# A two-layer encoder block: the order of the MLP's tiles, one pinned group of sums, and two diagonal matrices made earlier

## The chip, the cores and the metric

The kernel runs on one core of one Trainium2 chip, as one launch. The metric is the time of an execution in microseconds (us) on the device; the time before is the median of three runs. A profile is one further execution, recorded by the hardware profiler. Engines are named as in the profile: PE is TensorE (PEld its weight loads), DVE VectorE, ACT ScalarE, POOL GpSimd, SP the engine whose queue issues the loads of weights.

## What is computed

The reference is a stack of two layers over 256 tokens of width 2048. Each layer has an attention part and then an MLP; this case is about the MLP:

```
def sq_relu_mlp(h, g, w_in, w_out):
    return jnp.square(jax.nn.relu(rms_norm(h, g) @ w_in)) @ w_out

h = h + sq_relu_mlp(h, norm_mlp[layer], w_mlp_in[layer], w_mlp_out[layer])
```

`w_in` is 2048 x 8192 and `w_out` 8192 x 2048, all in fp32. `rms_norm` divides each token by the root of its mean square (plus 1e-6) and multiplies by a gain.

## The kernel before

**Precision.** Every fp32 operand is split into a high part, rounded by ACT (a cast to `float32r`), and a low part, the rest, which DVE subtracts. A product then takes three matmuls: high by high, high by low, low by high. Weights arrive as units of 128 x 1024 fp32 (512 KB, one DMA on SP's queue), are cast (hi) and subtracted (lo), and wait in rotating buffers: 6 raw, 4 hi, 5 lo. `weights()` hands out the next unit and prepares units ahead (`AHEAD = 3`), in the order of a list, `stream`, which is built from the same steps as the work. The lines of the splits are L171 and L174 (plain units, of up tiles), L225 and L226 (of sevens, with L220 to L224 as sums of the blocks first), L247 and L248 (of direct pairs).

**The MLP in steps.** The 8192 hidden features are four chunks of 16 tiles of 128. An up tile (a step "U" with its number, `features_major`) makes one tile of a chunk: 16 wide matmuls of 512 columns (high weights by both parts of the activations) and 16 narrow ones of 256 columns (low weights), all into one PSUM bank. Then `up` empties the bank: L449 on ACT copies one half, L1169 on DVE adds the other. `finish` follows: L1151 (DVE, ReLU and the tokens' inverse root), L1154 (ACT, square), and the split into `hid` by L1109 (ACT) and L1110 (DVE). For odd tiles below ten `block_sums` also forms sums of blocks (L1132 to L1135) and splits them.

The down projection of a chunk is two groups (n = 0 and 1), each of two column groups of 512. In a group, tiles 0 to 9 are taken two at a time by a seven ("S0" to "S4"): seven products in place of eight, Strassen's scheme in Winograd's form, 21 matmuls. Tiles 10 to 15 are taken directly: "A5" to "A7" for the first column group, "B5" to "B7" for the second, 12 matmuls each; A6 reads the tiles 12 and 13. A group has eight sums in PSUM: 11, 21 and 12 in the pool `acc` (four banks, the fourth is for up tiles), p1, p5 and 22 in a pool of two, p6 and p7 in pools of one. When the last product of a sum is in, it is copied or added (L1075, L1077) to sums in SBUF: four final ones per group, and `e`, the stored products of p1 with p6, p5 and p7.

**What sets the order.** `TURNS` writes the order of the steps by hand. The first string is the turn of group 0, in which the rest of the same chunk's up tiles is made; the second is the turn of group 1, in which the next chunk's first ten are made. The first string runs four times in a layer, the second three times (the last chunk's second group is computed afterwards by `tokens_major` or `features_major`). All TensorE instructions are kept in this order. For the other engines the framework simulates the program's time when it is built and orders each engine's instructions by that, so one that has its operands early can float ahead of where the program has it. `pin(ins)` keeps an instruction behind the one that the program has just before it on its engine: an order, not a wait.

**Side work.** A step ends in one or two calls of `slot()`, which advances each generator in `active` to its next `yield`. `merged(n)` adds the stored products of group n to the final sums, six additions of 128 x 512 (L1022), two to a slot; `merged(1)` is started in the last chunk before B5 (L1204), `merged(0)` by `merge_first` after the last step. `turned` then transposes the sums on TensorE and adds them to the residual stream (L1006). `inverse_root`, started four slots into the MLP, computes the inverse root of each token's mean square: two small matmuls (`stat`), a power on POOL (L553), two yields, then two diagonal matrices `dg` by DVE (L559), each followed by a matmul that spreads its diagonal over all partitions (`inv`, L560), and the copy `ri` that L1151 reads (L562).

Of the kernel before, what the change touches and what calls it, by code (L numbers as in the profile page):

```python
# [9 lines left out]
F32 = mybir.dt.float32  # L10
F32R = mybir.dt.float32r
AF = mybir.ActivationFunctionType
ALU = mybir.AluOpType
# [3 lines left out]
P = 128  # L17
D = 2048
T = 256
# [26 lines left out]
SEVEN = 5  # L46
ALONE = 10
TURNS = (
    "U10 S0 U11 S1 U12 A5 S2 U13 S3 A6 U14 S4 U15 B5 B6 A7 B7",
    "U0 S0 A5 U1 S1 A6 U2 S2 A7 U3 U4 S3 U5 U6 S4 U7 B5 U8 B6 U9 B7",  # L50
)


# [50 lines left out]
def trunk(  # L104
# [17 lines left out]
    nc = Engines(tc)  # L122
# [8 lines left out]
    nar = ctx.enter_context(tc.tile_pool(name="nar", bufs=6))  # L131
# [15 lines left out]
    ident = const.tile([P, P], F32, name="ident")  # L147
    make_identity(tc.nc, ident[:])
    neg_ones = const.tile([P, P], F32, name="neg_ones")
# [137 lines left out]
    def mm(o, lhs, rhs, start, stop):  # L287
        nc.tensor.matmul(o, lhs, rhs, start=start, stop=stop)
# [164 lines left out]
    def pin(ins, pinned=True):  # L453

        if pinned:
            tc.keep_in_program_order(ins)
# [88 lines left out]
    def inverse_root(acc, name):  # L545

        ps = ps_y.tile([P, 512], F32, name="stat", tag="y")
        for m in range(2):
            mm(ps[:, 2 * m : 2 * m + 2], acc[:, m * P : (m + 1) * P], neg_ones[:, 0:2], True, True)
        ms = tiny.tile([P, 4], F32, name="ms", tag="t4", bufs=8)  # L550
        nc.vector.tensor_scalar(ms[:], ps[:, 0:4], -1.0 / D, EPS, op0=ALU.mult, op1=ALU.add)
        r = tiny.tile([P, 4], F32, name="root", tag="t4", bufs=8)
        nc.gpsimd.tensor_tensor(r[:], ms[:], neg_half[:], op=ALU.pow)  # L553
        yield
        yield
        ps = ps_y.tile([P, 512], F32, name="inv", tag="y")
        for m in range(2):
            dg = nar.tile([P, P], F32, name="dg", tag="nar")
            nc.vector.tensor_scalar_mul(dg[:], ident[:], r[:, 2 * m : 2 * m + 1])  # L559
            mm(ps[:, m * P : (m + 1) * P], neg_ones[:], dg[:], True, True)  # L560
        ri = const.tile([P, T], F32, name=f"ri_{name}", tag="ri")
        nc.vector.tensor_scalar_mul(ri[:], ps[:, :T], -1.0)  # L562
        inverses[name] = ri
# [415 lines left out]

    def mlp(l, xg_, sq, h, done):  # L980
        start_side(delayed(inverse_root(sq, f"mlp{l}"), 4))
        sums = [heads4(f"d{l}_{i}") for i in range(4)]

        def summed(m, g):

            return sums[2 * m + g // 2][:, (g % 2) * 512 : (g % 2 + 1) * 512]
# [3 lines left out]
        def product_sum(i, n):  # L990

            return extra[i][:, n * 512 : (n + 1) * 512]
# [18 lines left out]
        def merged(n):  # L1011

            u, p5, p7 = (product_sum(i, n) for i in range(3))
            for i, (dst, src) in enumerate((
                (summed(0, 2 * n + 1), u),
                (summed(0, 2 * n + 1), p5),
                (u, p7),
                (summed(1, 2 * n), u),
                (u, p5),
                (summed(1, 2 * n + 1), u),  # L1020
            )):
                nc.vector.tensor_tensor(dst, dst, src, op=ALU.add)  # L1022
                if i % 2 == 1:
                    yield

# [151 lines left out]
        def merge_first(staged=staged):  # L1177
            if l == 1:
                yield from turned(3, None)
            for i, (dst, src) in enumerate(staged or ()):  # L1180
                nc.vector.tensor_tensor(dst, dst, src, op=ALU.add)
                if i % 2 == 1:
                    yield
            yield from merged(0)
            yield from turned(0, done)
            yield
            yield from turned(1, done)

        groups = {}
        for c, n, kind, i in mlp_steps():  # L1190
            if kind == "H":
                halves_first(xg_, FIRST_UP, lambda f, b: up(0, f, b))
                continue
            if kind == "T":
                two_tiles(xg_, [lambda b, f=f: up(0, f, b) for f in (i, i + 1)])
                continue
            if kind == "U":
                width["last"] = "wide"
                features_major(xg_, lambda b, c=c, i=i: up(c, i, b))
                continue  # L1200
            if (c, n) not in groups:
                groups[c, n] = Group(c, n, chunks[c][1], staged if c == NCH - 1 else None)
            if (c, kind) == (NCH - 1, "B") and i == sevens:
                start_side(merged(1))  # L1204
            if kind == "S":
                groups[c, n].seven(i)
            else:
                groups[c, n].direct(i, "AB".index(kind) + 1)
# [217 lines left out]
```

## Time and profile before

| | us |
|---|---|
| median of three runs | 2193.57 (2192.35 to 2194.9) |
| the profiled execution, its own time | 2191.9 |
| its span, first to last instruction | 2190.2 |
| PE busy | 2156.7 |
| DVE busy | 1743.2 |
| ACT busy | 1248.8 |
| MLP of the first layer, from its first up tile to its last matmul | about 435 to 1125 |
| MLP of the second layer | about 1483 to 2187 |

A row of the waits view reads: the waiting engine, its tile and line, the awaited engine, tile and line, then the idle time in all, how often, and the longest. All matmuls carry the line of a wrapper, L75, so they are told apart by tiles: `acc<-mlpx,hi` and `acc<-mlpx,lo` are the wide and narrow halves of up tiles, `acc<-hi,hid` and its like belong to sevens and direct pairs. A row of the timeline reads: start, duration, engine, line, operation, tiles, shape, count, and in brackets the engine's idle time before it and what ended that. Matmuls are pipelined: one of 512 columns lasts 0.39 us, and the next starts well before it ends. Times in a view are us from the span's start.

### The profile page before, as it was taken

How to read it: one execution, taken by the hardware profiler on the slowest of the kernel's cores; microseconds unless marked ns; L12 is line 12 of the kernel's file. 1: busy time of each engine (PE TensorE's matmuls, PEld its weight loads, DVE VectorE, ACT ScalarE, POOL GpSimd, SP SyncE). 2: the span in 40 equal slices, each digit the busy share in tenths (PEclk: the TensorE clock that was granted, in tenths of full speed). 3: DMA queues.
4: the chain of work that ended last, by engine and by line, in shares of the span. 5: the costliest groups of instructions: out<-in, count | busy, mean ns of one | idle time of the engine just before them, and what ended most of it. 6: DMA issues, size and time to landing. Idle time of an engine off the chain costs nothing.

```text
span 2190.2 us, 30309 instructions
## 1 busy us (share of the span) xinstructions
PE 2156.7 (98%) x11038; PEld 1841.7 (84%) x11038; DVE 1743.2 (80%) x2603; ACT 1248.8 (57%) x1828; POOL 205.2 (9%) x223
## 2 busy tenths in 40 slices
PE   9999999999999999999999999999999999999999
PEld 8888888888888888888888888888888888888887
DVE  7778886679888898899885556566988888888985
ACT  7644445456666555565555447555666656555563
POOL 0010112500000000000050112361000000000000
PEclk9999999999999999999999999999999999999999
DMA  9655556655665666656756654465665665666574
GB/s 330 194 162 184 172 182 197 194 176 182 197 211 182 198 189 197 201 188 183 207 175 192 191 188 130 135 190 181 188 203 185 197 193 191 194 193 211 164 218 129
DMA packets 213317, 414.65 MB, mean 189 GB/s; under 512 B 13232, under 2 KB 144304, under 8 KB 213168
## 3 DMA queue, kind: packets, MB, share of 16 engines
q1 hardware_dynamic: 212592, 410.63, 60.6%
q10 hardware_dynamic: 576, 2.10, 0.3%
q8 instruction: 86, 1.41, 0.3%
q14 instruction: 63, 0.52, 0.1%
HBM read 410.58 MB, written 2.10 MB: 188 GB/s over the span
## 4 chain that ended last, share of the span: by engine, by line
PE 93%; DVE 4%; issue 1%; DMA 1%; ACT 1%; DVEq 0%; ACTq 0%
PE acc L75 88%; PE accs L75 1%; PE yp L75 1%; DVE lo L226 1%; DVE lo L174 1%; PE tp L75 1%; DMA raw<-in_w_down 1%; PE s L75 1%; PE z L75 1%; DVE lo L248 0%; DVE raw L220 0%; ACT hi L225 0%; DVE up L1169 0%; DVE d L1022 0%; PE cold L75 0%
## 5 line engine op out<-in xcount | busy, mean ns | idle before, releaser
L174 DVE TENSOR_TENSOR lo<-raw,hi 128x1024 fp32r<-128x1024 f32 (+1 forms) x524 | 639.5, 1236 | 242.2 <-ACT hi L171 211.9
L171 ACT CAST hi<-raw 128x1024 fp32r<-128x1024 f32 (+1 forms) x524 | 541.4, 1043 | 345.0 <-PE acc L75 296.2
L75 PE MATMUL acc<-mlpx,hi 128*128 128x512 f32 x2048 | 485.5, 390 | 12.2 <-DVE up L1169 12.2
L75 PE MATMUL acc<-hi,hid 128*128 128x512 f32 x1404 | 473.6, 391 | 7.5 <-DVE hid L1110 6.7
L75 PEld LDWEIGHTS acc<-mlpx,hi 128*128 128x128 f32 x2048 | 382.7, 188 | 93.3 <-DVE up L1169 14.6
L225 ACT CAST hi<-raw 128x1024 fp32r<-128x1024 f32 (+1 forms) x280 | 264.5, 945 | 217.8 <-DVE raw L221 120.4
L226 DVE TENSOR_TENSOR lo<-raw,hi 128x1024 fp32r<-128x1024 f32 (+1 forms) x280 | 302.9, 1087 | 50.5 <-ACT hi L225 38.8
L75 PEld LDWEIGHTS acc<-hi,hid 128*128 128x128 f32 x1404 | 263.4, 188 | 63.5 <-DVE hid L1110 10.1
L75 PE MATMUL acc<-lo,hid 128*128 128x512 f32 x702 | 274.4, 391 | 0.0
L75 PEld LDWEIGHTS acc<-mlpx,lo 128*128 128x128 f32 x2048 | 261.3, 191 | 9.0
L75 PE MATMUL acc<-mlpx,lo 128*128 128x256 f32 x2048 | 264.6, 283 | 0.0
L75 PE MATMUL acc<-hi,xg 128*128 128x512 f32 x640 | 208.4, 398 | 0.0
L75 PEld LDWEIGHTS acc<-lo,hid 128*128 128x128 f32 x702 | 132.2, 188 | 23.7
L247 ACT CAST hi<-raw 128x1024 fp32r<-128x1024 f32 x108 | 113.6, 1055 | 61.7 <-PE acc L75 51.8
L248 DVE TENSOR_TENSOR lo<-raw,hi 128x1024 fp32r<-128x1024 f32 x108 | 131.6, 1230 | 20.7 <-ACT hi L247 20.6
L449 ACT COPY low<-acc 128x256 f32<-128x256 f32 x188 | 69.5, 370 | 137.7 <-PE acc L75 135.1
L75 PEld LDWEIGHTS acc<-hi,xg 128*128 128x128 f32 x640 | 120.2, 188 | 24.6
L75 PE MATMUL acc<-lo,xg 128*128 128x512 f32 x320 | 124.7, 390 | 0.7 <-DVE lo L174 0.7
L75 PE MATMUL acc<-y,hi 128*128 128x512 f32 x512 | 119.9, 391 | 0.0
L75 PEld LDWEIGHTS acc<-y,hi 128*128 128x128 f32 x512 | 95.0, 188 | 19.1
L75 PE MATMUL acc<-hi,s_w 128*128 128x512 f32 x280 | 98.1, 390 | 0.5 <-ACT hi L225 0.5
L1154 ACT ACTIVATE up<-up 128x256 f32<-128x256 f32 x128 | 52.6, 414 | 48.9 <-DVE up L1151 48.9
(211 smaller groups left out, 2612.7 us busy)
## 6 DMA issues: line engine op xcount, KB each, us to landing
raw<-in_w_up SPq DMA_DIRECT2D x256, 512.0 KB, 4.8
raw<-in_w_down SPq DMA_DIRECT2D x256, 512.0 KB, 5.6
raw<-in_w_in SPq DMA_DIRECT2D x80, 512.0 KB, 3.7
raw<-in_w_o SPq DMA_DIRECT2D x64, 512.0 KB, 4.0
raw<-in_w_mem SPq DMA_DIRECT2D x28, 512.0 KB, 6.1
raw<-in_w_kv_v SPq DMA_DIRECT2D x24, 512.0 KB, 3.9
raw<-in_w_kv_k SPq DMA_DIRECT2D x24, 512.0 KB, 4.2
raw<-in_w_q SPq DMA_DIRECT2D x24, 512.0 KB, 4.2
```

What stands on the lines that cost most here:

```text
L75: return self._tc.keep_in_program_order(fn(*args, **kwargs))
L171: nc.scalar.copy(hi[:, :n], raw[:, :n])
L174: nc.vector.tensor_tensor(lo, raw, hi.bitcast(F32), op=ALU.subtract)
L225: nc.scalar.copy(hi4, src)
L226: nc.vector.tensor_tensor(lo4, src, hi4.bitcast(F32), op=ALU.subtract)
L247: nc.scalar.copy(hi4, turned)
L248: nc.vector.tensor_tensor(lo4, turned, hi4.bitcast(F32), op=ALU.subtract)
L449: nc.scalar.copy(low[:], bank[:, T:])
L1154: nc.scalar.activation(a[:], a[:], AF.Square)
```

## The change

Three edits.

1. `TURNS`. In the first turn A6 and U14 change places. In the second turn the up tiles are spread so that a seven, a direct pair or two stand between any two of them; the steps are the same ones. The list of loads follows the steps, so it changes with them.
2. `inverse_root` makes both diagonals into one tile of 128 x 256 and yields twice before the two matmuls that read them. The diagonals stay in the slot in which they were; the matmuls and `ri` come two slots later.
3. The six additions of `merged` are pinned.

```
-    "U10 S0 U11 S1 U12 A5 S2 U13 S3 A6 U14 S4 U15 B5 B6 A7 B7",
-    "U0 S0 A5 U1 S1 A6 U2 S2 A7 U3 U4 S3 U5 U6 S4 U7 B5 U8 B6 U9 B7",
+    "U10 S0 U11 S1 U12 A5 S2 U13 S3 U14 A6 S4 U15 B5 B6 A7 B7",
+    "U0 S0 U1 A5 U2 S1 U3 A6 U4 S2 U5 A7 U6 S3 U7 S4 U8 B5 U9 B6 B7",
...
         yield
         yield
+        dg = nar.tile([P, T], F32, name="dg", tag="nar")
+        for m in range(2):
+            w = slice(m * P, (m + 1) * P)
+            nc.vector.tensor_scalar_mul(dg[:, w], ident[:], r[:, 2 * m : 2 * m + 1])
+        yield
+        yield
         ps = ps_y.tile([P, 512], F32, name="inv", tag="y")
         for m in range(2):
-            dg = nar.tile([P, P], F32, name="dg", tag="nar")
-            nc.vector.tensor_scalar_mul(dg[:], ident[:], r[:, 2 * m : 2 * m + 1])
-            mm(ps[:, m * P : (m + 1) * P], neg_ones[:], dg[:], True, True)
+            w = slice(m * P, (m + 1) * P)
+            mm(ps[:, w], neg_ones[:], dg[:, w], True, True)
...
-                nc.vector.tensor_tensor(dst, dst, src, op=ALU.add)
+                pin(nc.vector.tensor_tensor(dst, dst, src, op=ALU.add))
```

## The prediction

> **What bounds the kernel now.** I read the page first, then the waits of TensorE, then the stretches of the timeline in which those waits lie.
>
> ```profile
> span 2190.2 us, 30309 instructions
> PE 2156.7 (98%) x11038; PEld 1841.7 (84%) x11038; DVE 1743.2 (80%) x2603; ACT 1248.8 (57%) x1828; POOL 205.2 (9%) x223
> ```
>
> TensorE has a matmul in flight for 2156.7 of 2190.2 us. Only 33.5 us are left in which it has none, so an edit that touches no arithmetic can win at most about that. The view of the waits says whose they are (waiter, awaited, idle us in total, times, longest):
>
> ```profile
> PE acc L75 <- DVE up L1169: 12.2, 12, 1.4
> PE acc L75 <- DVE hid L1110: 6.7, 8, 0.9
> PE acc L75 <- DVE lo L226: 4.4, 4, 1.4
> ...
> PE inv L75 <- DVE dg L559: 1.8, 2, 0.9
> ...
> PE acc L75 <- ACT hid L1109: 0.8, 1, 0.8
> ...
> PE acc L75 <- ACT hi L225: 0.5, 2, 0.3
> ```
>
> All six belong to the MLP, and the counts name places in TURNS. "U3 U4" and "U5 U6" stand in the second turn, which runs three times in each of two layers: twelve. "S3 A6" stands in the first turn, four times in each layer: eight. The rest is the start of the last chunk and the start of each MLP. Idle time understates each loss, as the next rows show; they are TensorE's timeline (start, duration, what, idle before).
>
> ```profile
> 540.93 3.79 PE L75 MATMUL acc<-mlpx,hi 128*128 128x512 f32 x16
> 544.55 2.08 PE L75 MATMUL acc<-mlpx,lo 128*128 128x256 f32 x16
> 546.47 0.40 PE L75 MATMUL acc<-hi,hid 128*128 128x512 f32 x1
> ...
> 627.79 2.07 PE L75 MATMUL acc<-mlpx,lo 128*128 128x256 f32 x16
> 630.80 1.42 PE L75 MATMUL acc<-mlpx,hi 128*128 128x512 f32 x5 [0.94 <-DVE up L1169]
> ```
>
> An up tile takes 5.54 us from start to start (540.93 to 546.47), its narrow half 1.92. Between U5 and U6 the narrow half is followed by the next tile only after 3.01: 1.09 us lost for 0.94 idle. I add 0.15 to each idle gap.
>
> **Part 1: no two up tiles adjacent.** A down group holds three of the four banks named acc (11, 21, 12), so all up tiles share the fourth, and the next one waits until L449 (ACT) and L1169 (DVE) have emptied it. With a direct pair or a seven between, that wait has cover. Removed: 12.2 + 12 x 0.15 = 14.0 us. What is late next? The new second turn has a single direct between up tiles at four places (U1 A5 U2, U3 A6 U4, U5 A7 U6, U8 B5 U9): 4 x 3 x 2 = 24 places. Before has this at U7 B5 U8, U8 B6 U9 and U9 B7 U10, 18 places, none of which stalls. The tightest of them, and the slowest emptying of a bank once the turns run, where a seven gave it time:
>
> ```profile
> 992.49 0.40 PE L75 MATMUL acc<-hi,hid 128*128 128x512 f32 x1
> ...
> 995.24 3.79 PE L75 MATMUL acc<-mlpx,hi 128*128 128x512 f32 x16
> ```
>
> ```profile
> 994.78 0.42 DVE L1169 TENSOR_TENSOR up<-acc,low 128x256 f32<-128x256 f32 x1
> ...
> 2092.24 0.41 DVE L1169 TENSOR_TENSOR up<-acc,low 128x256 f32<-128x256 f32 x1
> ```
>
> ```profile
> 2089.49 0.40 PE L75 MATMUL acc<-hi,hid 128*128 128x512 f32 x1
> ```
>
> U7 ends and B5 begins at 992.49, U8 begins at 995.24: a direct covers 2.75 us. The bank was emptied at 994.78 + 0.42 = 995.20, after 2.71, just in time. The slowest one needed 2092.65 - 2089.49 = 3.16, so a new place costs between 0 and 0.41 us, the 24 between 0 and 9.8. I take 1, since the 18 places of the same form show 0.
>
> **Part 2: A6 one step later.** A6 reads hid of tile 13, which L1110 finishes late. Rows of TensorE (S3 begins where U13 ends) and of DVE, last chunk of the first layer:
>
> ```profile
> 1054.55 0.40 PE L75 MATMUL acc<-hi,hid 128*128 128x512 f32 x1
> ```
>
> ```profile
> 1062.15 0.41 DVE L1110 TENSOR_TENSOR hid<-up,hid 128x256 fp32r<-128x256 f32 x1
> ```
>
> From the end of U13 to its hid are 1062.56 - 1054.55 = 8.0 us. So far only S3 (4.79, a row below) lies between; after the change S3 and U14 do, 4.79 + 5.54 = 10.3. Even this slowest case has 2.3 us to spare. Removed: 6.7 + 8 x 0.15 = 7.9, and the one wait for L1109, which is the same place, 0.8 + 0.15 = 1.0. The cost is that U14's two weight units must be ready 2.7 us sooner and A6's one later; ACT, DVE and the SP queue see the same units in a slightly other order. POOL has none of it.
>
> **Part 3: merged sums pinned.** The sums of group 1 (L1022, started in the program at B5 of the last chunk) need only results of the chunk before, and the scheduler floats them ahead:
>
> ```profile
> L1022 DVE TENSOR_TENSOR d<-d,e x4: 680/682/683, 1011.5 to 1018.6; 128x512 f32<-128x512 f32 x4
> L1022 DVE TENSOR_TENSOR e<-e,e x2: 682/682/683, 1013.8 to 1017.1; 128x512 f32<-128x512 f32 x2
> ```
>
> Six sums of 0.68 us, 4.1 us, right ahead of S0 of the last chunk. The windows view (start:end, length, then busy us of PE, PEld, DVE, ACT, POOL with instructions; clock; DMA share; GB/s) has that S0 in either layer, a plain seven, then S0 U11 S1 of the second chunk and a longer stretch:
>
> ```profile
> 1017.35:1025.64 8.29, 5.84 (x23) 3.79 (x22) 7.51 (x12) 5.88 (x8) 0.00 (x0) 1.00 0.29 70
> 1031.18:1035.97 4.79, 4.79 (x24) 3.95 (x22) 4.76 (x7) 4.48 (x6) 0.00 (x0) 1.00 0.59 131
> 2065.34:2073.62 8.28, 5.84 (x24) 3.79 (x22) 7.50 (x12) 5.88 (x8) 0.00 (x0) 1.00 0.27 68
> 671.67:686.78 15.11, 15.11 (x76) 12.81 (x75) 14.83 (x20) 11.16 (x15) 0.00 (x0) 1.00 0.60 171
> 671.00:758.00 87.00, 86.17 (x430) 73.10 (x430) 78.28 (x100) 50.98 (x66) 0.00 (x0) 1.00 0.67 200
> ```
>
> The stalled S0 takes 8.29 instead of 4.79, with DVE busy 7.51 of it. Without the 4.1 us of sums DVE has more than the 3.5 us that it was late. Removed: 3.50 + 3.49 = 7.0 (this holds the waits for L226 and L225). The sums go to the slots of B5, B6 and A7, two at each. There DVE waits for casts:
>
> ```profile
> 1084.23 1.22 DVE L248 TENSOR_TENSOR lo<-raw,hi 128x1024 fp32r<-128x1024 f32 x1 [1.45 <-ACT hi L247]
> 1085.37 0.42 DVE L1110 TENSOR_TENSOR hid<-up,hid 128x256 fp32r<-128x256 f32 x1
> 1086.95 1.23 DVE L248 TENSOR_TENSOR lo<-raw,hi 128x1024 fp32r<-128x1024 f32 x1 [1.16 <-ACT hi L247]
> ```
>
> A pair fits into 1.45. Queued behind it on DVE would be the hid of tile 15, for which A7 waits: 0 to 1.3 us per layer. I take 0.3, 0.6 in all. The pin is an order on DVE alone, and the operands are long there, so it adds no semaphore wait.
>
> **Part 4: diagonals ahead.** TensorE waits for dg, which DVE runs behind a split:
>
> ```profile
> 455.24 0.68 PE L75 MATMUL inv<-dg,neg_ones 128*128 128x128 f32 x4 [0.88 <-DVE dg L559]
> ```
>
> ```profile
> 454.82 0.47 DVE L559 TENSOR_SCALAR dg<-ident,root 128x128 f32<-128x128 f32 x2
> ...
> 457.40 1.10 DVE L1151 SCALAR_TENSOR_TENSOR up<-up,ri_mlp 128x256 f32<-128x256 f32 x3
> ```
>
> The DVE work stays; its matmuls move two slots later, two runs of 16 wide ones at 3.62 us (540.93 to 544.55), 7.2 us, so dg is done long before. Removed: 1.8 + 2 x 0.15 = 2.1. The inverse arrives 7 us later too, and the three L1151 behind it, 1.1 us of DVE work, run later, in a stretch that leads to the first S0 at 498 us. Bounds 0 to 1.1 per layer; I take 0.2, 0.4 in all, as 40 us lie between.
>
> **Sum.** 14.0 + 7.9 + 1.0 + 7.0 + 2.1 = 32.0 us removed; 1 + 0.6 + 0.4 = 2.0 added, and 0.4 for S3 U7 S4 (rival B). Net 29.6. The profiled execution took 2191.9 us, 1.7 more than its span; that gives 2162.3. The median of the runs, 2193.57, lies 1.67 above the profiled one; I keep that distance and predict 2164.0 us.
>
> **Rival A, slower: the one bank for up tiles.** If the schedule puts L449 or L1169 behind two splits at each U-direct-U place, every one stalls. It loses from the point at which a place costs (32.0 + 4.4) / 24 = 1.5 us, which means emptying a bank in 2.75 + 1.5 = 4.25; at 1.7 us it costs 41, 2193.6 - 32.0 + 41 = 2203. For it: 2.71 of 2.75 are used already at 995. Against: the worst of all is 3.16.
>
> **Rival B, partial: DVE becomes the bound.** Old S3 U5 U6 S4 becomes S3 U7 S4. The same pattern, S0 U11 S1, has DVE busy 14.83 of 15.11 us without loss, but U7, an odd tile below ten, also makes block sums:
>
> ```profile
> L1110 DVE TENSOR_TENSOR s_w<-s,s_w 128x256 fp32r<-128x256 f32 x15 | 6.2, 417 | 0.0
> L1135 DVE TENSOR_TENSOR s<-up,s 128x128 f32<-128x128 f32 x15 | 4.2, 282 | 0.0
> ```
>
> Four of about 0.28, a split of 0.42 and one of 0.28: 1.8 us. So 16.6 against 15.1 us, and 1.5 us must come out of units split ahead. If nothing does, 1.5 x 3 x 2 = 9 us: 2173. I count 0.4 us in all, since U6 and U8 beside it make none.
>
> [...]
>
> **Rival C: the pin does not hold.** If the sums still run ahead of S0, 7.0 stay: 2171. Against it: the program starts them at B5, 70 us later.
>
> **Rival D: every gain comes back** as new waits in other places of the rescheduled DVE queue: no change.
>
> **How the numbers follow.** Forecast, 2160 to 2170: 0.68. B, 2170 to 2186: 0.15. C: 0.06. D: 0.04. A: 0.07. The low end has all 32.0 removed at no cost (2161.6) less the 1.2 us by which the runs scatter: 2160. The high end takes in C and B's 9 us with part of a bank cost: 2178; about 0.17 is left out. About 0.2%, 4.4 us, is what a measurement of this kernel can tell. Faster 0.68 + 0.15 + 0.06 = 0.89, same 0.04, slower 0.07.
>
> **What would show it.** In the waits of TensorE, "up L1169" (12), "hid L1110" (8) and "inv" are gone; S0 of the last chunk takes about 4.8 us; L1022 of group 1 starts after 1050 us; the span is near 2160.6 us. A is right if waits for L1169 return at U-direct-U; B if waits for L226 stand in S4 of the second turn. It is wrong if the listed waits go and the span does not fall.

## The result and the profile after

| | before | after |
|---|---|---|
| median, us | 2193.75 (2192.35 to 2194.9, 4 runs) | 2158.55 (2158.02 to 2159.2, 4 runs) |
| profiled execution, us | 2191.9 | 2158.02 |
| its span, us | 2190.2 | 2156.3 |

The ratio is 0.984, 95% interval 0.9823 to 0.9857: 35.2 us faster by the medians, 33.9 by the spans. One further execution of the kernel before, among those that ran beside the single edits below, took 2685.33 us at a granted clock of 0.752 and is left out of every figure. The forecast was 2164.0 and its low end 2160, so the time lies 1.45 us below the range. Lines of the changed kernel stand five further down: its L1027, L1082, L1115 and L1174 are L1022, L1077, L1110 and L1169 of before. The page after, and its waits of TensorE:

```profile
span 2156.3 us, 30341 instructions
...
PE 2148.9 (100%) x11038; PEld 1841.2 (85%) x11038; DVE 1745.1 (81%) x2603; ACT 1248.3 (58%) x1828; POOL 205.5 (10%) x223
```

```profile
PE tp L75 <- DVE h L1011: 2.2, 2, 1.1
PE cold L75 <- DVE zeros L142: 1.1, 1, 1.1
PE acc L75 <- DVE lo L174: 0.7, 1, 0.7
```

The 33.5 us without a matmul have become 7.4, and all six rows that the prediction listed are gone; the rows that are left were there before. Weight loads, DVE and ACT are busy for as long as they were. The windows after show S4 of the second turn in the third chunk, then S0 of the last chunk in either layer:

```profile
975.53:980.74 5.21, 5.07 (x23) 3.87 (x22) 5.21 (x8) 4.88 (x7) 0.00 (x0) 1.00 0.40 108
1005.59:1010.37 4.78, 4.78 (x23) 3.95 (x22) 4.78 (x7) 4.48 (x7) 0.00 (x0) 1.00 0.35 117
2036.05:2040.83 4.78, 4.78 (x23) 3.95 (x22) 4.78 (x7) 4.48 (x7) 0.00 (x0) 1.00 0.40 116
```

S0 takes 4.78 us where it took 8.29 and 8.28. The pinned sums, which ran from 1011 us on, now start at 1064.5, at the end of the chunk (four of them are of this form; the other two of the row belong to group 0):

```profile
L1027 DVE TENSOR_TENSOR d<-d,e x6: 675/682/689, 1064.5 to 1078.7; 128x512 f32<-128x512 f32 x6
```

One new delay came, where rival B put it: that S4 takes 5.21 instead of 4.79 us. DVE's timeline after shows why:

```profile
977.02 0.68 DVE L1082 TENSOR_TENSOR e<-acc,e 128x512 f32<-128x512 f32 x1
977.62 0.68 DVE L1082 TENSOR_TENSOR d<-acc,d 128x512 f32<-128x512 f32 x1
978.22 1.22 DVE L226 TENSOR_TENSOR lo<-raw,hi 128x1024 fp32r<-128x1024 f32 x1
```

Two additions of p1, which is complete after S4's first products, run right ahead of the split that S4's last step waits for. Such delays are 0.22 and 0.43 us in the second and third chunk of the first layer, 0.24 and 0.43 in the other, 1.3 in all.

### The profile page after: what moved, and what is told of

Same layout as the page of the kernel before. It is cut to its first block, busy times and chain, and to the rows that moved or that the text cites. A ratio compares the mean times of both kernels' runs of the same rounds, so it can differ in the third digit from the quotient of the medians.

```text
span 2156.3 us, 30341 instructions
## 1 busy us (share of the span) xinstructions
PE 2148.9 (100%) x11038; PEld 1841.2 (85%) x11038; DVE 1745.1 (81%) x2603; ACT 1248.3 (58%) x1828; POOL 205.5 (10%) x223
## 4 chain that ended last, share of the span: by engine, by line
PE 98%; DVE 2%; issue 0%; ACT 0%; DVEq 0%
PE acc L75 93%; PE accs L75 1%; PE yp L75 1%; PE tp L75 1%; PE s L75 1%; PE z L75 1%; DVE lo L226 0%; PE cold L75 0%; DVE lo L174 0%; DVE pt L654 0%; DVE lo L248 0%; ACT hi L171 0%; DVE h L1011 0%; PE stat L75 0%; DVE raw L223 0%
```

## The experiments

Theory M: the change removes the stalls that the prediction lists, and a stall costs TensorE more than its idle gap, about 0.3 us more in all. Theory P: the price that the prediction used, gap plus 0.15. Rival R: the gain comes from a DVE order that is new as a whole, so single edits do not add up to it.

**Each edit alone**, in the kernel before. For the second turn:

```
-    "U0 S0 A5 U1 S1 A6 U2 S2 A7 U3 U4 S3 U5 U6 S4 U7 B5 U8 B6 U9 B7",
+    "U0 S0 U1 A5 U2 S1 U3 A6 U4 S2 U5 A7 U6 S3 U7 S4 U8 B5 U9 B6 B7",
```

> The kernel before with the new second turn alone (up tiles of the second turn not adjacent). Theory M (the parts add, and a stall costs its gap plus about 0.29 us, 0.13 of that in the tile behind it): 12 waits for L1169 gone, worth 15.7, less 1.3 us in S4 of the second turn, so about 14.4 us faster; A6, S0 of the last chunk and inv stall as before. Theory P (the prediction's price, gap plus 0.15): 12.7 us faster with the same S4. Rival R (the gain came from a DVE order that is new as a whole, so parts do not add): the stall of S0 in the last chunk shrinks too, and it is 18 us or more faster.

The first turn alone (A6 and U14 change places):

> The kernel before with the new first turn alone (A6 behind U14). M: the eight waits for hid of tile 13 are gone, 1.12 us each and 2.26 in one, about 10.1 us faster. P: 8.9 us faster. R: an amount that does not fit the sum, under 6 or over 13.

The pin alone (`pin(...)` around L1022):

> The kernel before with the pinned sums alone. M and P: S0 of the last chunk falls from 8.29 to about 4.8 us in both layers, 7.0 us faster; nothing else moves. R: less than 4 us, since the floated sums would be late elsewhere, or nothing, since DVE is behind in S0 anyway.

The diagonals alone:

> The kernel before with the diagonals two slots ahead alone. M: the two waits before inv are gone, 1.1 us each, 2.2 us faster. P: 1.7 to 2.1 us faster. R: nothing, or slower, because the inverse arrives 7 us later and pushes DVE work towards the first S0.

| edit alone | median, us | against 2192.8 | ratio, 95% | span, us | against 2190.2 |
|---|---|---|---|---|---|
| second turn | 2184.88 | -7.9 | 0.9956 (0.9943 to 0.9969) | 2178.6 | -11.6 |
| first turn | 2185.10 | -7.7 | 0.9964 (0.9951 to 0.9977) | 2183.1 | -7.1 |
| pin | 2187.37 | -5.4 | 0.9972 (0.9961 to 0.9983) | 2186.5 | -3.7 |
| diagonals | 2189.90 | -2.9 | 0.9986 (0.9977 to 0.9995) | 2188.3 | -1.9 |

The kernel before has a median of 2192.8 us beside these runs. The medians add up to 23.9 us and the spans to 24.3, where the whole change gives 35.2 and 33.9: the edits need one another. M's and P's numbers for the two turns and the pin were not reached, by median or span; the diagonals came near both. R said that the parts would not add up, and they do not, but its amounts were missed for the turns and the diagonals. Each edit removes its own rows from the waits, and what it falls short of M by stands at a few places: the first three edits leave or open something else. The windows of the second turn alone have S0 of the last chunk in three pieces, the first two of one layer:

```profile
1011.23:1015.70 4.47, 2.73 (x12) 1.70 (x10) 4.47 (x9) 2.25 (x4) 0.00 (x0) 1.00 0.00 0
1015.70:1019.10 3.40, 2.93 (x6) 1.82 (x6) 2.62 (x5) 2.35 (x3) 0.00 (x0) 0.51 0.48 146
2052.80:2061.90 9.10, 5.87 (x23) 3.79 (x22) 8.32 (x14) 5.83 (x8) 0.00 (x0) 1.00 0.22 63
```

The new turn alone makes this S0 longer, 9.1 for 8.28, and the column of the granted clock reads 0.51 in the second piece: TensorE ran at half clock for 3.4 us. Also, two A6 take 5.00 us here, where one did (4.99) before. By starts in TensorE's timelines, the edit's 15.8 us less 1.3 in S4, 1.7 in the two S0 and 1.2 in A6 are 11.6, the difference of the spans. The first turn alone leaves S0 of the first layer as it was; in the second layer a stretch at half clock begins within S0, twice as long:

```profile
2056.58:2062.30 5.72, 4.07 (x17) 2.56 (x15) 4.96 (x9) 3.31 (x6) 0.00 (x0) 1.00 0.14 20
2062.30:2069.10 6.80, 6.29 (x14) 4.64 (x15) 6.67 (x8) 3.45 (x4) 0.00 (x0) 0.50 0.75 233
```

There S0 takes 9.32 us and the tile behind it 7.09 instead of 5.54, 2.6 more than before: 10.1 - 2.6 = 7.5, near the 7.1 of the spans. With the pin alone S0 is cured, but in the first layer the sums push the hid of tile 15 back; DVE's timeline there:

```profile
1081.88 0.69 DVE L1022 TENSOR_TENSOR e<-e,e 128x512 f32<-128x512 f32 x1
1083.11 1.23 DVE L248 TENSOR_TENSOR lo<-raw,hi 128x1024 fp32r<-128x1024 f32 x1 [0.55 <-ACT hi L247]
1084.26 0.68 DVE L1022 TENSOR_TENSOR d<-d,e 128x512 f32<-128x512 f32 x1
1084.86 0.42 DVE L1110 TENSOR_TENSOR hid<-up,hid 128x256 fp32r<-128x256 f32 x1
```

A7 began at 1081.83 and waited for that hid, which is the cost that the prediction bounded by 1.3 us; the waits are 1.21 us for ACT's half of the hid and 0.71 for DVE's, and with a half-clock stretch behind them (3.40 us at 0.51) A7 lasted 6.65 us instead of 2.72. That takes back 3.9 of the 7.0 us. In the whole change the sums come in another order with the casts, and A7 does not wait.

**The change without the pin.**

```
-                pin(nc.vector.tensor_tensor(dst, dst, src, op=ALU.add))
+                nc.vector.tensor_tensor(dst, dst, src, op=ALU.add)
```

> The changed kernel with the six sums not pinned. M: S0 of the last chunk stalls again, near 3.5 us in each layer, about 7 us slower than the changed kernel. Rival R: the new turn finishes U9 earlier (two directs and U10 lie between it and S0), so DVE is less behind and S0 stalls by under 1 us even with the sums ahead: under 2 us slower.

2170.87 us, ratio to before 0.9899 (0.9884 to 0.9915): 12.3 us above the changed kernel, more than M's 7, and R's 2 is out. Windows of this kernel: S0 of the first layer, then S0 of the second and part of the tile behind it, cut where the clock falls.

```profile
1006.16:1015.31 9.15, 5.92 (x24) 3.80 (x23) 8.37 (x14) 5.88 (x8) 0.00 (x0) 1.00 0.21 61
2041.05:2047.70 6.65, 4.20 (x18) 2.59 (x16) 5.88 (x12) 3.38 (x6) 0.00 (x0) 1.00 0.14 22
2047.70:2054.50 6.80, 6.31 (x14) 4.64 (x15) 6.70 (x8) 3.38 (x4) 0.00 (x0) 0.50 0.77 235
```

S0 loses 4.36 us in the first layer (9.15 - 4.79). In the second layer S0 takes 10.18 and the tile behind it, partly at half clock, 7.11 instead of 5.54: 7.0 lost. Together these are 11.3 of the 11.9 us between the spans. So the two stalls of S0 cost 7.0 in the old order and, with the half clock, 11.3 in the new one, in which DVE has 8.37 us of work within S0 where it had 7.51.

**Adjacent pairs doubled**, in the changed kernel:

```
-    "U0 S0 U1 A5 U2 S1 U3 A6 U4 S2 U5 A7 U6 S3 U7 S4 U8 B5 U9 B6 B7",
+    "U0 S0 U1 U2 A5 S1 U3 U4 A6 S2 U5 U6 A7 S3 U7 U8 S4 B5 U9 B6 B7",
```

> The changed kernel with four adjacent pairs of up tiles in each second turn (U1 U2, U3 U4, U5 U6, U7 U8), 24 in all, twice as many as before the change. M: 24 waits for L1169, each 1.24 us, 29.8 us, less the 1.3 of S4: about 28.5 us slower than the changed kernel. P: 24 x 1.09 = 26.2, less 1.3, 24.9 slower. If the idle gap alone were the cost: 24 x 0.94 - 1.3 = 21 slower.

2185.71 us (ratio to before 0.9965, 0.9952 to 0.9978), span 2184.9. Its waits view:

```profile
PE acc L75 <- DVE up L1174: 22.2, 24, 0.9
```

The span is 28.6 us above the changed kernel's, as M had it (28.5; P 24.9, the gap alone 21); by medians it is 27.2, still nearest to M. There is no wait in S4, so 24 stalls cost 28.6 + 1.3 = 29.9, 1.25 each (1.19 by medians), for an idle gap of 0.93. Where the other 0.3 goes shows in TensorE's timeline of before, U3 and then U4:

```profile
606.84 3.79 PE L75 MATMUL acc<-mlpx,hi 128*128 128x512 f32 x16
...
613.66 3.96 PE L75 MATMUL acc<-mlpx,hi 128*128 128x512 f32 x16 [1.12 <-DVE up L1169]
```

About half lies ahead of the gap, and the prediction counted it: without a stall the next tile starts 1.92 us after the narrow half does, but the narrow half lasts 2.07 or 2.08, and the view counts idle time only from its end. The rest lies in the tile behind, whose 16 wide matmuls take 3.96 instead of 3.79.

**What makes S4 late.** Two edits of the changed kernel. The first puts an even tile, which makes no block sums, between S3 and S4:

```
-    "... U5 A7 U6 S3 U7 S4 U8 B5 U9 B6 B7",
+    "... U5 A7 S3 U6 S4 U7 B5 U8 B6 U9 B7",
```

> The changed kernel with its second turn ending U5 A7 S3 U6 S4 U7 B5 U8 B6 U9 B7: between S3 and S4 lies U6, an even tile, which makes no block sums. If the block sums of an odd tile are what makes S4 late (rival B of the prediction), the waits of 0.21 and 0.42 us in S4 go and it is about 1.3 us faster than the changed kernel. If the additions of the stored products behind S4 make it late, S4 keeps them and nothing changes.

2165.0 us (ratio to before 0.9869, 0.9855 to 0.9883), 6.5 slower than the changed kernel, which neither case expected: S4 loses 0.95 to 1.31 in all six second turns. With no block sums ahead of it S4 is later, so they are not the cause. In DVE's timeline the two additions stand ahead of the split again:

```profile
803.30 0.69 DVE L1082 TENSOR_TENSOR e<-acc,e 128x512 f32<-128x512 f32 x1
803.91 0.68 DVE L1082 TENSOR_TENSOR d<-acc,d 128x512 f32<-128x512 f32 x1
804.50 1.22 DVE L226 TENSOR_TENSOR lo<-raw,hi 128x1024 fp32r<-128x1024 f32 x1
```

The second edit pins these additions:

```
-                        nc.vector.tensor_tensor(dst, src, dst, op=ALU.add)
+                        pin(nc.vector.tensor_tensor(dst, src, dst, op=ALU.add), q[0] == "p")
```

> The changed kernel with the additions of the stored products to their sums (p1, p5, p6, p7) pinned too. If the waits of 0.21 and 0.42 us in S4 of the second turn come from two additions of p1 that DVE runs ahead of the split for which S4 waits, they go: 1.3 us faster than the changed kernel. If block sums of U7 are the cause (rival B of the prediction), they stay, and a pinned addition can also be late for the bank of 22: no gain or slower.

The waits in S4 are gone, so the additions are shown to be the cause, but the time is the same, 2159.01 us (0.9839, 0.9825 to 0.9852), as A7 of the first layer now takes 1.9 us longer, for the same wait as with the pin alone. From its waits view:

```profile
PE acc L75 <- ACT hid L1114: 1.2, 1, 1.2
```

**Two sets of transposes in one slot.** In the run `both` the turn of `even` and the second set of transposes (column group 2) one slot later:

```
-        start_side(turned(g, done))
+        start_side(delayed(turned(g, done), 1 if g == 2 else 0))
```

> The turn of the run named even, and the transposes of column group 2 started one slot later, so that no slot holds two sets of transposes for the one bank of ps_t. If the two waits of 1.3 us before tp come from two sets in one slot, they go: 2.6 us faster than the run named even, and up to 3.9 faster than the changed kernel. If tp waits for DVE work however it is placed, no gain.

2164.09 us (0.9865, 0.9851 to 0.9879), 0.9 less than `even`, not 2.6: the wait goes in the first layer; in the second layer two sets now meet in two slots (1.1 and 0.8 us idle) instead of one. So the next run does it in the first layer alone, upon `pinp`:

> The run named pinp, and in the first layer alone the transposes of column group 2 one slot later. Expected: the wait for L1011 of 1.3 us in the first layer goes as well; 1.3 us faster than pinp, about 2155.9 us.

2158.01 us (0.9835, 0.9821 to 0.9848), 1.0 below `pinp` for the 1.3 expected; as `pinp` had gained nothing, 2155.9 was missed.

**How long a stall halves the clock.** In the changed kernel, after each pair of key tiles of the second layer, a tiny matmul that nothing uses waits for the tile just finished; `gap_b` puts three POOL operations more into that chain (n below is 0 in `gap_a` and 3 in `gap_b`).

```
+        late = keys_b[hd + 1][:, :P]
+        for _ in range(n):
+            link = nar.tile([P, P], F32, name="link", tag="nar")
+            nc.gpsimd.tensor_tensor(link[:], late, late, op=ALU.mult)
+            late = link[:]
+        probe = ps_y.tile([P, 512], F32, name="probe", tag="y")
+        mm(probe[:, 0:2], late, neg_ones[:, 0:2], True, True)
```

> The changed kernel with six gaps made on purpose in the second layer's key projection: after each pair of key tiles TensorE runs a tiny matmul on the tile just finished and so waits for ACT, DVE and POOL, about 2 us each, alone in 11 us of dense matmuls. About 13 us slower than the changed kernel. Theory H1: the clock is halved only after an idle stretch as long as the halved one lasts (3.4 us); then the granted clock stays 1.000 in all executions. Theory H2: it is the share of idle time in a few us that counts, as in the stalled S0, where no single gap was over 1.7 us; then some executions show stretches at half clock and up to 1.7 us more for each.

> The same with three more POOL operations in each chain, so six gaps of about 4 us. Both theories expect stretches of half clock here, in most executions; by H1 not in all, as a gap must hold a whole stretch of 3.4 us. About 25 us slower than the changed kernel, and 1.7 us more for each stretch of 3.4 us at half clock.

2184.09 us (0.9956, 0.9944 to 0.9969) and 2199.53 us (1.0025, 1.0016 to 1.0035), 25.5 and 41.0 above the changed kernel; the gaps were longer than meant, 17.4 us in all in `gap_a` (the longest 3.6) and 26.0 in `gap_b` (5.0). The granted clock is 0.996 to 0.998 in the five executions of `gap_a` and 0.992 to 0.995 in the ten of `gap_b`. The profile of `gap_a`, its first three probes, then windows around the second and one that holds the gap ahead of the third:

```profile
1224.63 0.38 PE L75 MATMUL probe<-neg_ones,kb 128*128 128x2 f32 x2 [1.92 <-POOL kb L1334]
1240.22 0.38 PE L75 MATMUL probe<-neg_ones,kb 128*128 128x2 f32 x2 [3.57 <-POOL kb L1334]
1255.81 0.38 PE L75 MATMUL probe<-neg_ones,kb 128*128 128x2 f32 x2 [2.36 <-POOL kb L1334]
```

```profile
1236.60:1240.90 4.30, 0.73 (x5) 0.64 (x5) 2.56 (x3) 1.32 (x2) 0.72 (x1) 1.00 0.75 229
1240.90:1244.30 3.40, 3.40 (x10) 2.66 (x9) 0.00 (x0) 0.44 (x1) 0.00 (x0) 0.51 0.42 163
1253.00:1256.50 3.50, 1.14 (x10) 0.94 (x9) 1.83 (x4) 0.37 (x1) 2.25 (x2) 1.00 0.90 314
```

In this execution the gap of 3.57 us is followed by 3.40 us at half clock, and the matmuls behind all three gaps of 3.6 us are slow: 32 wide ones take 9.16 and 9.13 us where 32 take 7.44 elsewhere, and behind the last gap 8 take 3.41 (in `pairs` 8 take 1.98). Behind both gaps of 2.36 us 32 narrow ones take 4.08 us, for 3.99 elsewhere, and behind the gap of 1.92 us 16 take 2.15, as the next 16 do. By itself that would fit H1. But S0 of the second turn alone got its half-clock stretch behind a window of 4.47 us with 1.74 us of idle time in all, and S0 of the first turn alone behind one of 5.72 us with 1.65 (both windows stand above). Windows of the pin alone, A7 of the first layer, then of the first turn alone, S0 of the first layer:

```profile
1081.83:1085.30 3.47, 1.58 (x6) 0.67 (x4) 2.90 (x5) 1.77 (x3) 0.00 (x0) 1.00 0.98 310
1085.30:1088.70 3.40, 3.37 (x8) 2.69 (x9) 0.69 (x1) 0.00 (x0) 0.00 (x0) 0.51 0.77 228
```

```profile
1014.29:1022.58 8.29, 5.85 (x23) 3.80 (x22) 7.51 (x12) 5.87 (x8) 0.00 (x0) 1.00 0.30 74
```

A7 got its half-clock stretch behind 1.89 us of idle time. In none of the three is there a gap of 3.4 us, so H1 fails. H2 is nearer, since half clock came behind several short gaps in a few us; but the first turn alone kept its clock in S0 of the first layer, with 2.44 us idle in 8.29, and `gap_a` kept it with 2.36 idle in 3.50, more than the 1.89 in 3.47 of A7. So the amount of idle time does not by itself tell which stall is hit, and what else does is not shown by these runs.

**Both kernels on one chip once more, and the best version.** `best2` is `best` with the additions pinned in the first three chunks only (`q[0] == "p" and self.c < NCH - 1`).

> The changed kernel once more, beside the kernel before on one chip. The executions of the kernel before whose granted clock is 1.000 throughout should lie near 2192, 33.5 us above it; those with a clock of 0.999 or 0.998 should be 1 to 4 us above these. The changed kernel should show 1.000 in all, near 2158.5 us.

> The run named best, with the additions of the stored products pinned in the first three chunks only. If pinning them in the last chunk is what makes A7 wait for hid of tile 15 in the first layer (1.89 us in pinp and best), that wait goes and S4 of the second turn stays without one: about 2156 us. If the wait at A7 comes from the six pinned sums whatever else is pinned, it stays: 2158 us.

The changed kernel takes 2158.6 us again (0.9839, 0.9825 to 0.9852), at a mean clock of 1.000 in all five executions. The kernel before has four executions at 1.000 beside it (2192.3 to 2193.21) and five below; four of these take 2194.16 to 2196.11, as expected, but one, at 0.999, takes only 2192.45. `best2` takes 2156.08 (2155.47 to 2156.45; ratio to before 0.9828, 0.9814 to 0.9841), 2.5 us below it and the fastest of all. A7 and S4 both go without a wait, so it was the pins in the last chunk that held up A7 in `pinp` and `best`. Its whole waits view:

```profile
PE cold L75 <- DVE zeros L142: 1.1, 1, 1.1
PE tp L75 <- DVE h L1011: 1.1, 1, 1.1
PE acc L75 <- DVE lo L174: 0.7, 1, 0.7
```

## Why the prediction was right and where it was wrong

The mechanism was right in all four parts: the stalls that it listed are those that went, at the places that the turns name, and S0 fell to a plain seven. The size was wrong, 5.4 us too small; three terms explain 5.2 of it.

**The price of a stall (3 us).** "I add 0.15 to each idle gap" is the step that failed. The tile behind a stall is slow too (16 wide matmuls in 3.96 for 3.79 us), and `pairs` puts the price at 0.3 beyond the gap. Measured from start to start in the profile of before, the twelve adjacent tiles lose 14.1 us up to the second tile's first matmul and 1.6 within it, 15.8 for the prediction's 14.0; A6 lasts 3.84 instead of 2.72 at seven places and 4.99 at one, 10.1 for 8.9; S0 is 7.0, as forecast; `inv` about 2.2 for 2.1. That is about 35 instead of 32.0. The low end of the range took 32.0 for the most that could go, so the time fell below it. The ceiling in its first paragraph ("can win at most about that", 33.5) fails by the same step: only 26.1 us of idle time went (33.5 - 7.4), and the span fell by 33.9.

**The added costs (1.1 us).** Of 2.4 us allowed, the bank of the up tiles, A7 and the later inverse cost nothing, and S4 cost 1.3 where 0.4 stood. Rival B named the right place with a wrong reason: the additions of p1, not the block sums, stand in the way. 35.0 - 1.3 = 33.7 for the 33.9 of the spans; the last 0.2 is not traced.

**The distance of the median (1.1 us).** "I keep that distance" carried the 1.67 us between median and profile of before over to the changed kernel, whose median lies 0.53 above its profile. Beside the single edits, the kernel before had 9 executions with a mean clock of 1.000, median 2192.07, and 7 with 0.998 or 0.999, median 2195.2. So its median holds executions at a lower clock, and its profile has none. By the clean ones the change is worth 2192.07 - 2158.55 = 33.5, close to the difference of the spans. In the profile of before, no 3.4 us, the length of the shorter half-clock stretches, hold more than 1.68 us of idle time, but for the slowest A6 (1.71): these are S0 of the last chunk, in both layers. In the changed kernel no 3.4 us up to the last matmul hold more than 1.12, and all nine executions ran at 1.000. That the stalled S0 can bring such a stretch is shown by the profiles of single edits; no profile of the kernel before caught one, so which of its stalls did is not shown.

**What was not seen.** The prediction priced each part by itself. That its sum came near was luck in so far as all parts were made together: the second turn alone makes S0 and an A6 longer, and the pin alone makes A7 wait. Rivals A and C did not come: no wait for L1174 is left, and the sums stay where they are pinned. Rival D, gains that come back as new waits, came in part, in the single edits alone. DVE's share only rose, from 80 to 81%, while 33.9 us went.

## What to carry to other kernels

Where one engine is nearly always busy, list its idle gaps by place and count, and match the counts with the order of the program; a stall costs more than its idle gap (1.25 us for 0.93 in `pairs`), so price it from the start of the work before it to the start of the work behind the slowed tile. Price an edit of the order together with its neighbours, since work that is moved off one deadline lands ahead of another. When executions of one kernel fall into two groups, look at the granted clock of each before taking a median as the size of an effect.

## What the runs showed of the hardware

A stall of a few us can cost more than its length. With the pin alone, waits of 1.21 and 0.71 us in A7 were followed by 3.40 us at a granted clock of 0.51, and A7 lasted 6.65 us instead of 2.72; in S0 of the first turn alone the clock was 0.50 for 6.80 us. In `gap_a` the three gaps of 3.57 and 3.58 us were followed by slow matmuls (32 wide ones in 9.16 us for 7.44), the gaps of 1.92 and 2.36 us were not. A stall may be hit or spared: S0 of the first turn alone was idle for 2.44 of 8.29 us in the first layer and kept a clock of 1.00; in the second layer half clock came behind 1.65 us of idle time in 5.72. Twenty-four gaps of 0.93 us, alone among dense matmuls, never did this: `pairs` ran at 1.000 in all five executions.
